# HGRN2 and short-convolution layer: diagonal blocks of A by identity products, and operands C in one run per partition

## The chip, the cores and the metric

The kernel runs on one core of one Trainium2 chip. The metric is the device time of one execution in microseconds (us), the median of several runs. Lower is better. The engines are TensorE (PE in the profile, with its weight loads as PEld), VectorE (DVE), ScalarE (ACT), GpSimd (POOL) and the queue that issues most DMAs (SP).

## What is computed

One layer works on 2048 tokens of width 1024, with 256 context tokens ahead of them. The tokens are normalised and modulated, and one input projection (1024 to 9216 columns) feeds two branches: a gated linear recurrence of 8 heads of width 128, run forward and backward, and a gated short convolution over rows of 64 tokens. Both go through one output projection. Cut to what matters here:

```python
def chunk_scan(q, k, v, logf, s0):                  # per head; chunks of tokens
    diff = bcum[:, :, :, None, :] - bcum[:, :, None, :, :]
    decay = where(mask, exp(where(mask, diff, 0)), 0)
    attn = einsum('bhtk,bhsk,bhtsk->bhts', qc, kc, decay)
    o = einsum('bhts,bhsv->bhtv', attn, vc) + einsum('bhtk,bhkv->bhtv', qc * exp(bcum), S)

p = h @ w_in[l]                                     # one projection for both branches
y = concatenate([hgrn_out(o, gate), conv_branch(p[..., HG_COLS:], conv_w, grid=True)]) @ w_out[l]
x = x + gate * y                                    # then a final RMSNorm
```

## The kernel before, in words

**Large products.** The projections run as products of f16 pairs (a high and a low part, three matmuls for one), put together after Strassen with 7 products instead of 8. A function `seven` issues the 7 products of a unit, `HK` = 4 k-tiles times 3 matmuls each. In the head windows a moving operand has 256 columns and comes from a tile `hop`; in the pair windows, where two token groups of 512 run together, it has 512 columns and comes from a tile `C[i][o]`, one for each of the 7 operands and 2 token halves.

**Order of the work.** Windows follow each other: 32 head windows (8 heads times 4 token groups, up to about 1262 us), 4 windows of the first convolution block, 14 pair windows for the other 7 blocks, then 8 output units. While a window's products are issued, the steps of other work (the scan of the segment of the window before, output steps of the head before, preparation of weights) are put between them by weights in a table `PACE`. The compiler's scheduler then sets the order on each engine from the program's order and its own account of when operands are there; each engine runs its queue in that order.

**A segment's scan.** A segment is 512 tokens (4 chunks of 128) of a head. Its attention matrix A is made in levels: at each level DVE multiplies decay totals into K (line 485) and Q (line 492), ACT and POOL keep mixed copies `km` and `qm` (lines 601 and 608), and PE makes blocks of A (line 631, 128x32 weights and 32 columns, 16 matmuls at a time). Levels 0 to 4 give the 32x32 diagonal blocks; DVE puts them together in a tile `Ac` of 128 partitions by 4 chunks by 32 (line 639). The step `level6` makes the last two levels in one PSUM bank `s.pt`: 16 matmuls of 64 columns for level 5 (line 650), which also write over the place of the diagonal blocks, and 16 for level 6 (line 657). ACT copies the bank to A (line 661), and POOL then copies the diagonal blocks out of `Ac` over it, 4 copies of 32 partitions (line 665). Two steps later the output products read A (line 737). Between them stand `key_turn` (transposes `kT` of K, line 672), `states` (products `T`, line 681) and, of the head before, output sums (line 777) whose banks come from the same pair of buffers as `kT`.

**Operands of the pair windows.** `load_C` loads each C by two DMAs, one for each token group (line 991). The source is 4096 bytes in one run per partition; the tile is laid out `[P, HK, 2, GW]`, so that a DMA writes 8 runs of 512 bytes in each partition. After the pair windows the same tiles hold the output weights (`wo_home`, `wo_at`, `load_wo`).

Of the kernel before, what the change touches and what calls it, by code (L numbers as in the profile page):

```python
# [10 lines left out]
F16 = mybir.dt.float16  # L11
# [8 lines left out]
P = 128  # L20
# [5 lines left out]
GW = 512  # L26
NG = SEQ // GW
NCH = GW // P
HK = KT // 2
HW = GW // 2  # L30
# [7 lines left out]
SB = 32  # L38
# [22 lines left out]
def hybrid_layer(ctx: ExitStack, tc, x, cx, w_ada, b_ada, w_in, w_out, fnorm_w, small_d, masks, ident_d, sel_d, out):  # L61
    nc = tc.nc
    V, S, G, PE, SY = nc.vector, nc.scalar, nc.gpsimd, nc.tensor, nc.sync
# [16 lines left out]
    OPS = ("B11", "T1", "T2", "B21", "T3", "B22", "T4")  # L80
# [3 lines left out]
    Hd = [{o: Hr[g][r][:, i] for r in ROWS for i, o in enumerate(r)} for g in range(NG)]  # L84
# [9 lines left out]
    def pa_t(nm):  # L94
        return pa.tile([P, 512], F32, tag="pa", name=nm)
# [4 lines left out]
    def ring(nm):  # L100
        return rp.tile([P, GW], F32, tag="ring", name=nm)
# [69 lines left out]
    ident = cp.tile([P, P], F32, name="ident")  # L171
# [335 lines left out]
    class Seg:  # L507
# [133 lines left out]
        def level6(s):  # L641

            n = s.n
            km, qm = s.kept
            s.pt = pa_t(f"A5_{s.nm}")
            for ch in range(NCH):
                for j in range(P // SB):
                    o = ch * P + j * SB
                    c0 = ch * P + j // 2 * 2 * SB
                    PE.matmul(s.pt[j * SB:(j + 1) * SB, c0:c0 + 2 * SB], km[:, o:o + SB], qm[:, c0:c0 + 2 * SB],  # L650
                              start=True, stop=True)
            for ch in range(NCH):
                for j in range(P // SB):
                    i = j // 2
                    o = ch * P + j * SB
                    t = ch * P + (1 - i) * 64
                    PE.matmul(s.pt[j * SB:(j + 1) * SB, t:t + 64], s.K[:, i * n + o:i * n + o + SB],
                              s.qf[:, (1 - i) * n + t:(1 - i) * n + t + 64], start=True, stop=True)
            s.update(6)
            s.A = ring(f"A_{s.nm}")  # L660
            S.activation(s.A, s.pt, AF.Copy)  # L661
            A3 = s.A.rearrange("p (c t) -> p c t", c=NCH)
            for j in range(P // SB):
                js = slice(j * SB, (j + 1) * SB)
                G.tensor_copy(A3[js, :, js], s.Ac[js])  # L665

        def key_turn(s):
            s.kT = []
# [300 lines left out]
    def finish_unit():  # L969
        while pending:  # L970
            pending.pop()()
        while afterwards:
            afterwards.pop(0)()


    late, ext = W(), W()
    late.rs = cp.tile([P, 33], F32, name="wrs")
    C = [{}, {}]
# [7 lines left out]
    def load_C(names, pool=None, tp=0):  # L986

        def one(o, j):
            if j == 0:
                C[tp][o] = (pool or ext.cr).tile([P, HK, 2, GW], F16, name=f"C{tp}{o}")  # L990
            SY.dma_start(C[tp][o][:, :, :, j * HW:(j + 1) * HW], Hd[2 * tp + j][o])

        return [lambda o=o, j=j: one(o, j) for o in names for j in range(2)]

# [13 lines left out]
    def settle(wk):  # L1008

        while any(j_[1] == wk for j_ in jobs):  # L1010
            for _ in jobs.pop(0)[2]:
                pass
# [13 lines left out]
    Wd = {o: dp.tile([P, 2, KT, GW], F16, name=f"Wd{o}", tag=f"Wd{o}") for o in OPS}  # L1026
# [32 lines left out]

    def wo_home(name, hl):  # L1060
        i = 2 * OPS.index(name) + hl
        return C[i // 7][OPS[i % 7]]

    def wo_at(name, hl, k):
        return wo_home(name, hl)[:, k // 2, k % 2, :]

    def load_wo(lo_, hi_):

        for i in range(lo_, hi_):
            SY.dma_start(wo_home(OPS[i // 2], i % 2).rearrange("p a k n -> p (a k) n"), Wd[OPS[i // 2]][:, i % 2])  # L1070

    Gr = dp.tile([P, GW], F32, name="Gr", tag="Gr")

# [124 lines left out]
    for hd in range(HEADS):  # L1198
# [4 lines left out]
        for i, g in enumerate(order(h.prim, NG)):  # L1203
            s = Seg(hd, g * GW, GW, 0, f"{hd}_{g}")
# [22 lines left out]
    for wi, (kind, a, i) in enumerate(stretch):  # L1227
# [69 lines left out]
        if kind == "head" and a >= 6:  # L1297
            n = (a - 6) * NG + i
            extra += [paced(0.2, lambda k=k: wo_scan(k)) for k in (2 * n, 2 * n + 1)]
        if kind == "pair":  # L1300
            n = (a - 1) * 2 + i
# [149 lines left out]
    ui = 0  # L1451

    def run(wi, units, steps):
# [20 lines left out]
        for un, (wk, kind, i, fn) in enumerate(units):  # L1474
            settle(wk)
            w = ws[wk]
            if not hasattr(w, "sx"):
                finish_w(w, f"w{ui}")
            final = turnover and kind != "ctx" and all(u[1] == "ctx" for u in units[un + 1:])
            def retire(wk=wk, at=ui):  # L1480
                if last[wk] == at:
                    next_w(wk[2], 4)

            if kind == "ctx":
                finish_unit()
                ps = bank(turn_bank[0], f"u{ui}")[:, :CTX]
                turn_bank[0] = 1 - turn_bank[0]
                for k in range(KT):
                    op, kk = w.ops[(("A11", "A12"), ("S1", "A22"))[i - 1][k // HK]], k % HK
                    r = k // HK * i  # L1490
                    PE.matmul(ps, op[0][:, kk], hc[:, r, 0, kk], start=k == 0, stop=False)
                    PE.matmul(ps, op[0][:, kk], hc[:, r, 1, kk], start=False, stop=False)
                    PE.matmul(ps, op[1][:, kk], hc[:, r, 0, kk], start=False, stop=k == KT - 1)
                    tick(1)
                fn(ps, w)
                retire()
            elif kind == "plain":
                ps = bank(turn_bank[0], f"u{ui}")
                turn_bank[0] = 1 - turn_bank[0]
                for half in range(2):  # L1500
                    hs = slice(half * HW, (half + 1) * HW)
                    for k in range(KT):
                        op, kk = w.ops[f"A{i}{k // HK + 1}"], k % HK
                        r = [plain[wi][k // 2][:, k % 2, hl, hs] for hl in range(2)]
                        PE.matmul(ps[:, hs], op[0][:, kk], r[0], start=k == 0, stop=False)
                        PE.matmul(ps[:, hs], op[0][:, kk], r[1], start=False, stop=False)
                        PE.matmul(ps[:, hs], op[1][:, kk], r[0], start=False, stop=k == KT - 1)
                        tick(1)
                fn(ps, w)
                retire()  # L1510
            elif kind == "pair":
                def pair_step(o, last_unit=ui == len(uses) - 1):
                    tick(2)
                    if o and last_unit and o != OPS[6]:
                        load_wo(7 + OPS.index(o), 8 + OPS.index(o))

                seven(w.ops.get, lambda o, hl, k, i=i: C[i][o][:, k, hl, :], HK, GW, f"{ui}", pair_step,
                      w.sx[:, 0:1], ring, retire, *fn(w))
            else:
                def step(o, final=final):  # L1520
                    tick(1)
                    if o and final:
                        freed[0] += 1
                        prefetch()

                seven(w.ops.get, lambda o, hl, k: hop[gw][o][:, k, hl, :], HK, HW, f"{ui}", step,
                      w.sx[:, 0:1], u_tile, retire, *fn(w))
            ui += 1
# [156 lines left out]
```

## Time and profile before

| | us |
|---|---|
| median of 3 runs | 2150.0 |
| lowest and highest of them | 2148.01, 2152.14 |
| the profiled execution | 2151.83 |
| its span, first to last instruction | 2150.1 |

A row of the profile gives an engine, a source line, what is written and read (out<-in), and times. In the timeline a group of equal instructions is one row with its count; an f32 matmul has two records, so that 16 of them show as x32. Durations of PE's instructions overlap, so what a group costs PE is read from its start to the start of the next. A wait is written as `[idle before <-releaser]`. The chain of work that ended last follows each instruction back to what released it.

### The profile page before, as it was taken

How to read it: one execution, taken by the hardware profiler on the slowest of the kernel's cores; microseconds unless marked ns; L12 is line 12 of the kernel's file. 1: busy time of each engine (PE TensorE's matmuls, PEld its weight loads, DVE VectorE, ACT ScalarE, POOL GpSimd, SP SyncE). 2: the span in 40 equal slices, each digit the busy share in tenths (PEclk: the TensorE clock that was granted, in tenths of full speed). 3: DMA queues.
4: the chain of work that ended last, by engine and by line, in shares of the span. 5: the costliest groups of instructions: out<-in, count | busy, mean ns of one | idle time of the engine just before them, and what ended most of it. 6: DMA issues, size and time to landing. Idle time of an engine off the chain costs nothing.

```text
span 2150.1 us, 53050 instructions
## 1 busy us (share of the span) xinstructions
PE 2073.2 (96%) x22111; PEld 1466.0 (68%) x22111; DVE 1645.8 (77%) x3413; ACT 1192.2 (55%) x2406; POOL 191.8 (9%) x272
## 2 busy tenths in 40 slices
PE   5988999999999999999999999999999999999998
PEld 2877878888888888888888887444444444444443
DVE  6787988878778787788687887678778656687775
ACT  7965666757567666576676654354445423333332
POOL 0121111111111110111110100000000000000000
PEclk9999999999999999999999999999999999999999
DMA  9567533442344233424543458933442105642421
GB/s 356 191 207 265 178 126 134 137 158 72 114 129 146 97 114 109 153 81 142 194 131 127 130 165 260 285 108 110 134 149 93 54 23 196 206 143 92 137 79 59
DMA packets 185798, 311.02 MB, mean 145 GB/s; under 512 B 13010, under 2 KB 114770, under 8 KB 183764
## 3 DMA queue, kind: packets, MB, share of 16 engines
q1 hardware_dynamic: 183396, 303.68, 42.9%
q8 instruction: 173, 2.83, 0.5%
q10 hardware_dynamic: 2160, 3.93, 0.5%
q14 instruction: 69, 0.57, 0.1%
HBM read 240.19 MB, written 67.37 MB: 143 GB/s over the span
## 4 chain that ended last, share of the span: by engine, by line
PE 65%; DVE 18%; ACT 7%; DMA 4%; issue 3%; POOL 1%; SPq 0%; POOLq 0%; ACTq 0%; DVEq 0%
PE sa L930 8%; PE sa L932 8%; PE sa L931 8%; PE sb L930 4%; PE sb L932 4%; PE sb L931 4%; PE sa_o L930 2%; PE sa_o L931 2%; PE sa_o L932 2%; DVE Q L492 2%; PE sc L930 2%; PE sc L931 2%; PE sc L932 2%; DVE K L485 2%; PE T L681 2%
## 5 line engine op out<-in xcount | busy, mean ns | idle before, releaser
L931 PEld LDWEIGHTS <-e_p 128*128 128x128 f16 x1332 | 130.4, 98 | 59.8 <-issue 10.3
L930 PEld LDWEIGHTS <-e_p 128*128 128x128 f16 x1332 | 130.4, 98 | 54.0 <-issue 1.1
L601 ACT ACTIVATE km<-K 128x512 f32<-128x512 f32 x192 | 129.6, 675 | 67.2 <-DVE K L485 61.1
L932 PEld LDWEIGHTS <-e_p 128*128 128x128 f16 x1332 | 130.3, 98 | 51.4
L485 DVE TENSOR_TENSOR K<-K,tot 128x512 f32<-128x512 f32 x192 | 132.2, 689 | 42.9 <-ACT km L601 25.3
L492 DVE TENSOR_TENSOR Q<-Q,tot 128x512 f32<-128x512 f32 x192 | 132.5, 690 | 34.9 <-POOL qm L608 19.5
L608 POOL COPY qm<-Q 128x512 f32<-128x512 f32 x96 | 80.8, 842 | 794.4 <-DVE Q L492 778.7
L931 PEld LDWEIGHTS <-whib_p 128*128 128x128 f16 x888 | 86.9, 98 | 42.1 <-issue 8.8
L930 PEld LDWEIGHTS <-whib_p 128*128 128x128 f16 x888 | 86.8, 98 | 36.7 <-issue 0.8
L930 PEld LDWEIGHTS <-whia_p 128*128 128x128 f16 x888 | 87.0, 98 | 35.7 <-DMA hop3B<-Hd3B 2.3
L932 PEld LDWEIGHTS <-wloa_p 128*128 128x128 f16 x888 | 87.0, 98 | 34.2
L931 PEld LDWEIGHTS <-whia_p 128*128 128x128 f16 x888 | 87.0, 98 | 33.9 <-issue 1.5
L932 PEld LDWEIGHTS <-wlob_p 128*128 128x128 f16 x888 | 86.8, 98 | 34.0
L157 ACT ACTIVATE e_p<-ws_p,sc_p 128x512 f16<-128x512 f32 x108 | 77.5, 718 | 54.9 <-DVE ws_p L444 42.0
L665 POOL COPY A<-Ac 32x128 f32<-32x128 f32 x128 | 77.2, 603 | 128.3 <-ACT A L661 110.6
L853 ACT ACTIVATE cv<-c,small 128x512 f32<-128x512 f32 (+1 forms) x36 | 24.2, 673 | 106.8 <-DVE c L871 61.1
L937 ACT ACTIVATE u<-sa,sx_w 128x256 f32<-128x256 f32 (+1 forms) x111 | 58.1, 524 | 43.5 <-PE sa L932 34.7
L937 ACT ACTIVATE p<-sa,sx_w 128x256 f32<-128x256 f32 (+1 forms) x111 | 57.4, 517 | 39.9 <-PE sa L932 39.8
L158 DVE SCALAR_TENSOR_TENSOR e_p<-ws_p,sc_p,e_p 128x512 f16<-128x512 f32 x108 | 79.4, 750 | 0.0
L409 ACT ACTIVATE junk<-ws_p 128x1024 f16<-128x1024 f32 x72 | 75.7, 1052 | 6.5 <-DMA ws_p<-in_w_in 6.3
L1596 POOL TENSOR_TENSOR x_o<-x_o,fw 128x512 f32<-128x512 f32 x1 | 1.3, 1262 | 868.0 <-ACT junk L1587 868.0
L937 ACT ACTIVATE p<-sb,sx_w 128x256 f32<-128x256 f32 (+1 forms) x111 | 57.8, 521 | 30.8 <-PE sb L932 28.0
(858 smaller groups left out, 7036.3 us busy)
## 6 DMA issues: line engine op xcount, KB each, us to landing
ws_p<-in_w_in SPq DMA_DIRECT2D x72, 512.0 KB, 4.3
y_o<-yT SPq DMA_DIRECT2D x32, 512.0 KB, 4.3
xt_x<-in_x SPq DMA_DIRECT2D x16, 512.0 KB, 6.2
wa<-in_w_ada SPq DMA_DIRECT2D x16, 512.0 KB, 10.2
Gd<-zs SPq DMA_DIRECT2D x32, 256.0 KB, 2.7
sg<-Gd SPq DMA_DIRECT2D x32, 256.0 KB, 4.4
wos<-in_w_out SPq DMA_DIRECT2D x32, 256.0 KB, 5.0
yT<-y SPq DMA_DIRECT2D x32, 256.0 KB, 2.9
```

The lines of the kernel that those rows point to most:

```text
L157: S.activation(hi, src, AF.Copy, scale=st[:, 0:1])
L158: V.scalar_tensor_tensor(lo, src, st[:, 0:1], hi, ALU.mult, ALU.subtract)
L409: S.activation(junk.rearrange("p (k n) -> p k n", k=KT), stage[i], AF.Abs, accum_out=r)
L485: V.tensor_tensor(m, m, sub(cur, nb + 1, [[2, np_], [-(nb + 1), 2], [0, B]]), ALU.mult)
L492: V.tensor_tensor(m, m, sub(cur, 1, [[2, np_], [nb - 1, 2], [0, B]]), ALU.mult)
L601: S.activation(sub(s.km, 0, [[2 * B, n // (2 * B)], [B, 2], [1, B]]), mix(s.K, n, B, n // (2 * B)), AF.Copy)
L608: G.tensor_copy(sub(qm, 0, [[2 * B, n // (2 * B)], [B, 2], [1, B]]), mix(s.qf, n, B, n // (2 * B)))
L665: G.tensor_copy(A3[js, :, js], s.Ac[js])
L930: PE.matmul(ps, hi[:, k], rh, start=start and k == 0, stop=False, skip_group_check=not start)
L931: PE.matmul(ps, hi[:, k], right(name, 1, k), start=False, stop=False, skip_group_check=not start)
L932: PE.matmul(ps, lo[:, k], rh, start=False, stop=k == nk - 1, skip_group_check=not start)
L937: last_keep.append(S.activation(r, ps, AF.Copy, scale=sx))
```

## The change

In `level6` 16 products are added behind those of line 657: columns `js` of the identity as weights, the chunk of `Ac` as moving operand, written into the bank over the diagonal blocks. ACT's copy of the bank then gives the whole of A, and the four copies on POOL are taken out. The tiles C are laid out `[P, 2, HK, 2, HW]`, with the token group outside, so that each DMA writes one run of 4096 bytes per partition; the moving operand of a pair product then is two runs of 256 columns. The views of the output weights in these tiles are rewritten for the new layout; their runs stay as they were.

```diff
@@ -656,13 +656,14 @@
                     t = ch * P + (1 - i) * 64
                     PE.matmul(s.pt[j * SB:(j + 1) * SB, t:t + 64], s.K[:, i * n + o:i * n + o + SB],
                               s.qf[:, (1 - i) * n + t:(1 - i) * n + t + 64], start=True, stop=True)
+            for ch in range(NCH):
+                for j in range(P // SB):
+                    js = slice(j * SB, (j + 1) * SB)
+                    PE.matmul(s.pt[js, ch * P + j * SB:ch * P + (j + 1) * SB], ident[:, js], s.Ac[:, ch], start=True,
+                              stop=True)
             s.update(6)
             s.A = ring(f"A_{s.nm}")
             S.activation(s.A, s.pt, AF.Copy)
-            A3 = s.A.rearrange("p (c t) -> p c t", c=NCH)
-            for j in range(P // SB):
-                js = slice(j * SB, (j + 1) * SB)
-                G.tensor_copy(A3[js, :, js], s.Ac[js])
 
         def key_turn(s):
             s.kT = []
@@ -987,8 +988,8 @@
 
         def one(o, j):
             if j == 0:
-                C[tp][o] = (pool or ext.cr).tile([P, HK, 2, GW], F16, name=f"C{tp}{o}")
-            SY.dma_start(C[tp][o][:, :, :, j * HW:(j + 1) * HW], Hd[2 * tp + j][o])
+                C[tp][o] = (pool or ext.cr).tile([P, 2, HK, 2, HW], F16, name=f"C{tp}{o}")
+            SY.dma_start(C[tp][o][:, j], Hd[2 * tp + j][o])
 
         return [lambda o=o, j=j: one(o, j) for o in names for j in range(2)]
 
@@ -1059,15 +1060,15 @@
 
     def wo_home(name, hl):
         i = 2 * OPS.index(name) + hl
-        return C[i // 7][OPS[i % 7]]
+        return C[i // 7][OPS[i % 7]].rearrange("p j k l n -> p (j k l n)").rearrange("p (k n) -> p k n", n=GW)
 
     def wo_at(name, hl, k):
-        return wo_home(name, hl)[:, k // 2, k % 2, :]
+        return wo_home(name, hl)[:, k, :]
 
     def load_wo(lo_, hi_):
 
         for i in range(lo_, hi_):
-            SY.dma_start(wo_home(OPS[i // 2], i % 2).rearrange("p a k n -> p (a k) n"), Wd[OPS[i // 2]][:, i % 2])
+            SY.dma_start(wo_home(OPS[i // 2], i % 2), Wd[OPS[i // 2]][:, i % 2])
 
     Gr = dp.tile([P, GW], F32, name="Gr", tag="Gr")
 
@@ -1514,7 +1515,7 @@
                     if o and last_unit and o != OPS[6]:
                         load_wo(7 + OPS.index(o), 8 + OPS.index(o))
 
-                seven(w.ops.get, lambda o, hl, k, i=i: C[i][o][:, k, hl, :], HK, GW, f"{ui}", pair_step,
+                seven(w.ops.get, lambda o, hl, k, i=i: C[i][o][:, :, k, hl, :], HK, GW, f"{ui}", pair_step,
                       w.sx[:, 0:1], ring, retire, *fn(w))
             else:
                 def step(o, final=final):
```

The order of PE at level 6 of the segment that the rows below show (head 2, group 0) was this, `hop9T` and `whib_p` being operands of the large products:

```order
L932 MATMUL sa_6430<-hop9T_6165,wlob_p_5603 128x256
L650 MATMUL A_2_0_6744<-qm_2_0_6727,km_2_0_6688 32x64 x16
L657 MATMUL A_2_0_6744<-Q_0_6221,K_0_5632 32x64 x16
L930 LDWEIGHTS whib_p_5602
L930 MATMUL sa_6430<-hop9T_6165,whib_p_5602 128x256
```

and is now this, with line numbers one higher behind the change:

```order
L933 MATMUL sa_6526<-hop9T_6261,wlob_p_5687 128x256
L650 MATMUL A_2_0_6840<-qm_2_0_6823,km_2_0_6784 32x64 x16
L657 MATMUL A_2_0_6840<-Q_0_6317,K_0_5716 32x64 x16
L662 MATMUL A_2_0_6840<-Ac_0_6607,ident 32x32 x16
L931 LDWEIGHTS whib_p_5686
L931 MATMUL sa_6526<-hop9T_6261,whib_p_5686 128x256
```

The new products stand right behind line 657, as in all 32 segments, and the large products follow them.

On DVE, behind the K and Q of that last level, stand the first instructions of the next segment (`Q_1`, `ks_1`, `K_1`, `tot_1`) and an output sum of the head before (`Q_3<-Q_3,o_1_3`, line 777). Before:

```order
L485 TENSOR_TENSOR K_0_5632<-K_0_5632,tot_0_6453 128x4x2x64
L492 TENSOR_TENSOR Q_0_6221<-Q_0_6221,tot_0_6453 128x4x2x64
L567 TENSOR_TENSOR Q_1_6790<-q_1_6429,f_1_6265 128x1024
L569 TENSOR_TENSOR ks_1_6792<-K_1_6266 128x512
L498 TENSOR_TENSOR tot_1_7001<-f_1_6265 128x512
L777 TENSOR_TENSOR Q_3_3842<-Q_3_3842,o_1_3_6819 128x512
L485 TENSOR_TENSOR K_1_6266<-K_1_6266,f_1_6265 128x256x2
```

Now:

```order
L485 TENSOR_TENSOR K_0_5716<-K_0_5716,tot_0_6549 128x4x2x64
L492 TENSOR_TENSOR Q_0_6317<-Q_0_6317,tot_0_6549 128x4x2x64
L569 TENSOR_TENSOR ks_1_6900<-K_1_6362 128x512
L567 TENSOR_TENSOR Q_1_6898<-q_1_6525,f_1_6361 128x1024
L485 TENSOR_TENSOR K_1_6362<-K_1_6362,f_1_6361 128x256x2
L498 TENSOR_TENSOR tot_1_7109<-f_1_6361 128x512
L778 TENSOR_TENSOR Q_3_3890<-Q_3_3890,o_1_3_6927 128x512
```

`K_1<-K_1,f_1` has moved ahead of the output sum, which is line 778 now; the same change of places is there in 6 segments. Beyond these, DVE has 40 evacuations of line 941 in other places (33 of them later, by one to three), 61 state sums of line 725 (53 later) and 65 multiplications of line 485 (42 earlier); ACT has 46 copies `km` in other places (39 earlier). PE's order is otherwise the same from the fourth head window on.

## Rows read from the trace of the kernel before

**Rows 1.** the page: engines' busy time, the chain's shares, two Pool groups

```profile
PE 2073.2 (96%) x22111; PEld 1466.0 (68%) x22111; DVE 1645.8 (77%) x3413; ACT 1192.2 (55%) x2406; POOL 191.8 (9%) x272
...
PE 65%; DVE 18%; ACT 7%; DMA 4%; issue 3%; POOL 1%; SPq 0%; POOLq 0%; ACTq 0%; DVEq 0%
...
L608 POOL COPY qm<-Q 128x512 f32<-128x512 f32 x96 | 80.8, 842 | 794.4 <-DVE Q L492 778.7
...
L665 POOL COPY A<-Ac 32x128 f32<-32x128 f32 x128 | 77.2, 603 | 128.3 <-ACT A L661 110.6
```

**Rows 2.** busy us by stretch: PE, PEld, DVE, ACT, POOL, granted clock, DMA

```profile
300.00:1262.00 962.00, 940.09 (x14476) 830.42 (x14475) 769.68 (x1696) 631.70 (x1426) 132.51 (x187) 1.00 0.39 128
...
1345.00:2150.00 805.00, 794.15 (x3682) 358.28 (x3679) 573.87 (x995) 313.42 (x478) 4.16 (x3) 1.00 0.38 124
```

**Rows 3.** what PE waited for, 300 to 1262 us: total us, times, longest us

```profile
PE A L631 <- POOL qm L608: 6.9, 8, 2.7
PE sa L930 <- ACT u L937: 3.3, 11, 0.6
PE A L631 <- DVE Q L492: 2.1, 8, 0.3
...
PE kT L672 <- DVE Q L777: 1.0, 4, 0.2
```

**Rows 4.** who waited for the copies of line 665: us, times

```profile
  POOL hpT_x L301: 2.0, 1
```

**Rows 5.** timeline of PE at level 0: start us, us, line, tiles, shape

```profile
422.93 0.46 PE L631 MATMUL A<-q,ks 128*32 128x32 f32 x32
423.20 0.56 PE L631 MATMUL A<-Q,km 128*32 128x32 f32 x32
423.70 0.28 PE L930 MATMUL sa<-hop9T,whib_p 128*128 128x256 f16 x1
```

**Rows 6.** timeline of PE at level 6 of the same segment

```profile
435.48 0.65 PE L650 MATMUL A<-qm,km 128*32 128x64 f32 x32
435.95 0.63 PE L657 MATMUL A<-Q,K 128*32 128x64 f32 x32
436.51 0.28 PE L930 MATMUL sa<-hop9T,whib_p 128*128 128x256 f16 x1
```

**Rows 7.** pieces of the chain behind level 6: start us, us, what

```profile
436.13 0.49 PE A L657 x32
...
436.64 0.69 DVE K L485
...
440.55 0.60 DVE Q L777
441.15 1.04 DVE K L485
```

**Rows 8.** timeline of PE after it, in brackets the wait and what ended it

```profile
441.20 0.66 PE L672 MATMUL kT<-ident,K 128*128 128x128 f32 x4 [0.25 <-DVE Q L777]
...
457.36 0.46 PE L631 MATMUL A<-qm,km 128*32 128x32 f32 x32 [0.46 <-POOL qm L608]
458.09 0.46 PE L631 MATMUL A<-Q,km 128*32 128x32 f32 x32 [0.27 <-DVE Q L492]
```

**Rows 9.** timeline of the SP queue at the last loads of C

```profile
1351.46 2.76 SPq L991 DMA_DIRECT2D C1T<-Hd3T  x1
...
1369.44 1.17 SPq L401 DMA_DIRECT2D ws_p<-in_w_in  x1
```

**Rows 10.** what PE waited for, 1262 to 2150 us, the longest

```profile
PE sa L930 <- DVE b L941: 0.9, 1, 0.9
```

**Rows 11.** timeline of Pool and DVE behind level 6

```profile
437.30 3.41 POOL L665 COPY A<-Ac 32x128 f32<-32x128 f32 x4 [3.63 <-ACT A L661]
...
439.09 0.77 DVE L569 TENSOR_TENSOR ks<-K 128x512 f32<-128x512 f32 x1
```

**Rows 12.** all of line 569: ns min/median/max, first and last start

```profile
L569 DVE TENSOR_TENSOR ks<-K x32: 676/688/1097, 72.7 to 1235.9; 128x512 f32<-128x512 f32 x32
```

## Prediction

> **What bounds the kernel now.** I read the page's busy shares and chain first, then busy time by stretch, then what TensorE waited for in each stretch, and last the timeline around one level 6 step. TensorE (PE) is busy for 2073.2 us of a span of 2150.1 us [rows 1]. By stretch it is busy for 940.09 of the 962 us from 300 us to the end of the head windows, and for 794.15 of the 805 us of the pair and output windows, at a granted clock of 1.00 in both [rows 2]. So PE sets the end, and work that is added to its queue costs its full length unless it falls into a wait that PE has anyway. Such waits are few: from 300 to 1262 us PE waits 6.9 us in 8 places for the Pool copy qm, 3.3 us in 11 for an evacuation u, 2.1 us in 8 for Q, and 1.0 us in 4 for Q of line 777 [rows 3]. The chain names PE with 65% and DVE with 18% [rows 1]: DVE is on it only in those few stretches that end in one of these waits.
>
> **Edit 1, what is removed.** 128 copies on Pool, 77.2 us [rows 1]. Nobody waits for them but one other Pool instruction, for 2.0 us once [rows 4]. The output products that read A come two steps later and don't wait for Pool at all. So this part is worth nothing by itself. What DVE may gain from a quieter Pool is a rival, below.
>
> **Edit 1, what is added.** 16 products per segment, 32 segments, 512 in all, on the engine that sets the end. They stand right behind the 16 products of line 657, with no wait of their own, since Ac's last write on DVE comes ahead of the K and Q that line 657 waits for. Their form is that of line 631 (128x32 weights, 32 columns, f32), and a group of 16 shows as x32 in the timeline. Two such groups back to back start 0.27 us apart, and the second holds PE for 0.50 us until the next f16 product [rows 5]; a group that followed a wait held it for 0.39 us [rows 8]. Today the products of line 650 hold PE for 0.47 us, those of line 657, which end the f32 stretch, for 0.56 us [rows 6]. With a third group behind them line 657 should take 0.47, as line 650 does, and the new group 0.39 to 0.50: 0.47 + 0.39 - 0.56 = 0.30, or 0.47 + 0.50 - 0.56 = 0.41. I take 0.35 us, and 0.27 and 0.41 as ends. Times 32 that is **11.2 us** (8.6 to 13.1), if all of it is on the path.
>
> **Edit 1, where it is not on the path.** In the segment shown, DVE's K of the last level starts at 436.64, when line 657's reads end [rows 7]; it doesn't wait for the new products. 4.7 us later PE stands 0.25 us at a transpose kT for the bank that DVE's line 777 frees, and 16 us after that 0.46 and 0.27 us at the levels of the next segment [rows 8]. Here DVE leads and PE follows, so 0.35 us more on PE would be swallowed. PE stands at kT like this in 4 places [rows 3], and the program has the sequence in 6 of its 32 segments (it shows in the order of DVE, above). In the others I count the full 0.35 us.
>
> **What the new order does.** The scheduler has moved more than the new products. At these same 6 places K times f, which holds DVE for 1.04 us behind line 777 now [rows 7], stands ahead of it in the new order. The bank is then freed about 1.0 us later, and PE's kT with it: 1.0 us instead of the 0.35 us above, some 0.7 us more, times 6: **+4.2 us**. Later PE arrives so late at the levels that about 0.5 us of the 0.73 us there [rows 8] is gone, in each of the 6: **-3 us**; I keep 0 to -4.4 as ends, since on ACT the scalings of line 825 also move and two more of them stand ahead of the second gate. Waits that don't hang on PE elsewhere (the T products for kT, the early segments) may swallow 0.3 us each in some 8 segments: **-2.5 us** (0 to -4). Many evacuations (line 941) and sums (line 725) stand one or two places later, levels earlier; no row shows a wait that this moves, so I count 0 with 3 us on either side.
>
> **Edit 2, the operands C.** The 28 loads carry the same bytes in one run per partition. The late ones keep the SP queue for up to 2.76 us each now, and a weight load behind them is issued at 1369.44 [rows 9]. It should get shorter to issue and to land. But PE's whole waiting from 1262 us on has one entry above 0.5 us, 0.9 us for an evacuation on DVE, and none for a load [rows 10]. So this gain is hidden: 0, at most a few tenths. On PE the moving operand is now two runs of 256 columns instead of one of 512, in 14 windows x 2 units x 7 x 12 = 2352 products. In runs of one element a group of 16 took 0.56 against 0.46 us [rows 5], 6 ns each with 31 breaks, 0.2 ns per break; in runs of four it took the same 0.46 us as in one run [rows 8]. Two runs are nearer to the latter: 0, at most 2352 x 0.2 ns = 0.5 us.
>
> **The sum.** 11.2 + 4.2 - 3 - 2.5 = +9.9 us against the profiled execution of 2151.8 us. I take +9, since the two last terms could be larger more easily than the first. The three timed runs have their median 1.8 us below the profiled one, so the forecast for the median is 2150.0 + 9 = **2159 us**. What a measurement of this kernel can tell from no change is about 0.2%, 4.3 us; the forecast lies at 0.4%.
>
> **Rivals.**
> *Swallowed.* The new products fall into waits that PE has anyway. For: 21.9 us of the 962 us are not busy by [rows 2], about as much as the products add twice over. Against: 3.3 us of them are for evacuations u [rows 3], which follow PE's own last product and move with it. It would give +0 to +4 us, 2150 to 2154.
> *The order costs more.* Where K or km now stands ahead of an evacuation, PE waits for a bank not at 6 places but in most segments. Upper ends of the terms: 13.1 + 4.2 + 3 + 0.5 = 20.8, so 2165 to 2171. For: PE has 3.3 us of waits for u in 11 places already [rows 3], so the slack there is short. Against: the evacuations that move behind km are mostly p5 of bank b, which is needed again only two products later.
> *Faster: DVE is freed from Pool's copies.* Line 569 took 0.77 us while the copies of line 665 ran, from 437.30 to 440.71 us [rows 11], and has a median of 0.688 us over all segments [rows 12]. 77 us of copies cover at most some 110 instructions of that size, 0.08 us each: 9 us less on DVE. If the whole of the waits for qm, Q and line 777 (6.9 + 2.1 + 1.0 = 10.0 us [rows 3]) went with that, and all of the products fell into what is left of the idle time (21.9 - 10.0 = 11.9 us), the end would be 2150 - 10.0 = 2140 us. It decides from the point where more than 15.5 us of PE's idle time go (11.2 us for the products, and 4.3 us). Against: line 569 was itself waited for by nobody, and Pool stands idle for 778.7 us in total ahead of its qm copies, waiting for DVE's Q [rows 1], so those waits are not Pool's making. On this the Trainium skill, "SBUF — State Buffer", section "Who interferes with whom", says that VectorE and GpSimd share one pair of ports by an exclusive lock; by "SBUF: two separate sides" of that page the loser blocks fully. By that rule the copies could hold DVE for up to their whole 77 us, and the kernel would come out on this rival's side; the rows bear out at most the 0.08 us.
> *The change is not felt where it says.* Edit 2 may reach nothing since no load is waited for; that is already my count, and what would speak against it is a time that falls although the products cost what they cost.
>
> **How the numbers follow.** Forecast (+4 to +14) 0.48; swallowed 0.20; the order costs more 0.22; faster 0.10. The most likely gives 2159. Leaving out the faster case and the far half of the costlier one, the range is 2149 to 2169. Faster by over 0.2%: 0.09; within: 0.24 (swallowed, and a little of the two beside it); slower: 0.67.
>
> **What the profile of the changed kernel would show.** Line 662 with x1024 records and the line after it some 0.35 us later than before; no Pool copy to A; kT waiting for line 778 in 6 places for about a microsecond; the waits for qm near 457 us gone or smaller; loads of C at 0.3 to 0.6 us of SP each; pair products of the same length as now. A stretch from 300 to 1262 us that is not 6 to 12 us longer would make the prediction wrong, as would a change in the length of the pair windows.

## The result, and the profile after

The changed kernel takes 2158.78 us (median of 5 runs, 2157.59 to 2160.03) where the kernel before takes 2150.0 us (5 runs, 2146.92 to 2152.14): a ratio of 1.0044, interval 1.0033 to 1.0055. It is slower by over 0.2%. The forecast was 2159.0 us. The profiled execution took 2158.78 us with a span of 2157.0 us, 6.9 us more than the span before.

From the page of the changed kernel, the engines' busy time, the chain's shares, and two groups (busy us, mean ns of one, then idle time before them and what ended it):

```profile
PE 2078.2 (96%) x23135; PEld 1477.2 (68%) x23135; DVE 1643.9 (76%) x3413; ACT 1191.5 (55%) x2406; POOL 115.1 (5%) x144
...
PE 67%; DVE 16%; ACT 8%; DMA 4%; issue 3%; POOL 1%; SPq 0%; POOLq 0%; ACTq 0%; DVEq 0%
...
L608 POOL COPY qm<-Q 128x512 f32<-128x512 f32 x96 | 79.5, 828 | 978.5 <-DVE Q L492 978.5
...
L662 PE MATMUL A<-Ac,ident 128*32 128x32 f32 x1024 | 15.3, 197 | 0.0
```

Beside [rows 1]: POOL has lost its 77 us of copies, and the identity products have their 1024 records with no idle time ahead of them. By stretch (columns as in [rows 2]) the head windows carry the change:

```profile
300.00:1262.00 962.00, 938.19 (x15138) 833.97 (x15140) 760.94 (x1679) 628.15 (x1421) 68.43 (x82) 1.00 0.39 127
1345.00:2157.00 812.00, 801.10 (x3721) 362.26 (x3719) 579.47 (x1016) 316.66 (x483) 4.16 (x3) 0.99 0.37 125
```

PE is busy 1.9 us less in the first stretch than in [rows 2], although it has more to do there: it waits more. What it waited for, 300 to 1262 us (total us, times, longest us):

```profile
PE A L631 <- POOL qm L608: 6.5, 6, 2.6
PE sa L931 <- ACT u L938: 3.8, 11, 0.7
PE vt_c L555 <- ACT vT_c L550: 3.5, 3, 1.2
PE kT L673 <- DVE Q L778: 2.4, 4, 0.6
PE A L631 <- DVE Q L492: 2.1, 8, 0.3
```

Against [rows 3], kT waits 2.4 us in place of 1.0, and a wait that the prediction doesn't have stands third: the turn of the context values `vt_c`, 3.5 us in 3 places. PE's timeline at level 6 of the segment that [rows 6] shows:

```profile
434.65 0.65 PE L650 MATMUL A<-qm,km 128*32 128x64 f32 x32
435.12 0.63 PE L657 MATMUL A<-Q,K 128*32 128x64 f32 x32
435.57 0.48 PE L662 MATMUL A<-Ac,ident 128*32 128x32 f32 x32
435.98 0.28 PE L931 MATMUL sa<-hop9T,whib_p 128*128 128x256 f16 x1
...
441.04 0.66 PE L673 MATMUL kT<-ident,K 128*128 128x128 f32 x4 [0.61 <-DVE Q L778]
```

From line 657's start to the next f16 product it is 435.98 - 435.12 = 0.86 us now, 0.56 in [rows 6]: a group of 16 costs 0.30 us. The last row answers to the first of [rows 8]: 0.61 us of wait in place of 0.25.

**A stretch for comparisons.** Whole times scatter by some us from run to run, so beside the medians I compare one stretch that all kernels have: from the first product behind level 6 of head 1's first segment to the same of head 6's first, 20 segments. In PE's timeline of the kernel before, of the changed kernel, of the kernel without diagonal blocks (e3) and of the one with both orders put back (e12, lines as in the changed kernel; e3's are 5 lower), its ends are:

```profile
290.69 0.28 PE L930 MATMUL sa<-hop5T,e_p 128*128 128x256 f16 x1
1015.32 0.28 PE L930 MATMUL sa<-hop25T,whib_p 128*128 128x256 f16 x1
```

```profile
289.21 0.28 PE L931 MATMUL sa<-hop5T,e_p 128*128 128x256 f16 x1
1018.94 0.28 PE L931 MATMUL sa<-hop25T,whib_p 128*128 128x256 f16 x1
```

```profile
289.06 0.28 PE L926 MATMUL sa<-hop5T,e_p 128*128 128x256 f16 x1
1011.41 0.28 PE L926 MATMUL sa<-hop25T,whib_p 128*128 128x256 f16 x1
```

```profile
290.51 0.28 PE L931 MATMUL sa<-hop5T,e_p 128*128 128x256 f16 x1
1016.13 0.28 PE L931 MATMUL sa<-hop25T,whib_p 128*128 128x256 f16 x1
```

That is 724.63 us before, and 729.73, 722.35 and 725.62 us then: +5.1, -2.3 and +1.0 us against before. The other kernels, read in the same way from one profiled execution each, stand in the table.

| kernel | median us | ratio to before, interval | 20 segments, against before, us |
|---|---|---|---|
| changed | 2158.78 | 1.0044 (1.0033 to 1.0055) | +5.1 |
| e1 products alone | 2158.86 | 1.0051 (1.0037 to 1.0064) | +4.9 |
| e2 layout alone | 2147.89 | 1.0000 (0.9991 to 1.0010) | -0.5 |
| e3 no diagonal | 2144.80 | 0.9985 (0.9976 to 0.9993) | -2.3 |
| e4 products and copies | 2163.55 | 1.0070 (1.0057 to 1.0083) | +8.1 |
| e5 products first, narrow | 2147.35 | 0.9988 (0.9979 to 0.9997) | -1.8 |
| e6 narrow | 2156.38 | 1.0033 (1.0021 to 1.0045) | +4.9 |
| e7 sum first | 2157.05 | 1.0031 (1.0018 to 1.0045) | +3.4 |
| e8 products twice | 2185.18 | 1.0159 (1.0142 to 1.0176) | +18.7 |
| e9 turn first | 2157.10 | 1.0034 (1.0023 to 1.0045) | +2.6 |
| e10 copies on ACT | 2153.09 | 1.0011 (1.0001 to 1.0021) | +1.9 |
| e11 narrow and copies | 2158.27 | 1.0039 (1.0026 to 1.0053) | +3.1 |
| e12 both orders | 2156.56 | 1.0034 (1.0020 to 1.0049) | +1.0 |

The kernel before, run beside each group, had medians of 2148.02 (e1 to e4), 2150.04 (e5 to e8), 2149.21 (e9 to e11) and 2150.18 us (e12).

### The profile page after: what moved, and what is told of

Same layout as the page of the kernel before. It is cut to its first block, busy times and chain, and to the rows that moved or that the text cites. A ratio compares the mean times of both kernels' runs of the same rounds, so it can differ in the third digit from the quotient of the medians.

```text
span 2157.0 us, 54885 instructions
## 1 busy us (share of the span) xinstructions
PE 2078.2 (96%) x23135; PEld 1477.2 (68%) x23135; DVE 1643.9 (76%) x3413; ACT 1191.5 (55%) x2406; POOL 115.1 (5%) x144
## 4 chain that ended last, share of the span: by engine, by line
PE 67%; DVE 16%; ACT 8%; DMA 4%; issue 3%; POOL 1%; SPq 0%; POOLq 0%; ACTq 0%; DVEq 0%
PE sa L931 8%; PE sa L933 8%; PE sa L932 8%; PE sb L931 4%; PE sb L932 4%; PE sb L933 4%; PE sa_o L931 2%; PE sa_o L933 2%; PE sa_o L932 2%; PE sc L931 2%; PE sc L932 2%; PE sc L933 2%; DVE Q L492 2%; PE A L631 2%; PE T L682 2%
## 5 line engine op out<-in xcount | busy, mean ns | idle before, releaser
L157 ACT ACTIVATE hiS_o<-y_o,sc_y 128x1024 f16<-128x1024 f32 x32 | 36.8, 1149 | 70.1 <-PE sa_o L932 32.1
L682 PE MATMUL T<-v,kT 128*128 128x128 f32 x512 | 64.2, 278 | 2.6 <-ACT kT L675 2.5
```

The lines of the kernel that those rows point to most:

```text
L157: S.activation(hi, src, AF.Copy, scale=st[:, 0:1])
L682: PE.matmul(pt[:, sl], s.kT[i][:, sl], s.v[:, sl], start=True, stop=True)
```

## Experiments: the two edits and the copies on POOL

The theory was the prediction's: the products cost their time on PE, the new order a few us, the copies on POOL and the layout nothing. The rivals: the layout matters, or POOL's copies hold DVE.

**e1 and e2, one edit at a time.** Of the changed kernel, e1 takes back the layout, e2 the first hunk:

```diff
-                C[tp][o] = (pool or ext.cr).tile([P, 2, HK, 2, HW], F16, name=f"C{tp}{o}")
-            SY.dma_start(C[tp][o][:, j], Hd[2 * tp + j][o])
+                C[tp][o] = (pool or ext.cr).tile([P, HK, 2, GW], F16, name=f"C{tp}{o}")
+            SY.dma_start(C[tp][o][:, :, :, j * HW:(j + 1) * HW], Hd[2 * tp + j][o])
...
```

Expected of e1: 

> The first edit alone (identity products in, copies on POOL out), C laid out as before; every engine's order is that of the changed kernel. Theory (the products' own time on PE makes the loss, the layout of C is worth nothing): 2157 to 2160, as the changed kernel's 2158.8. Rival (the two-run moving operand of the pair products costs something): 2152 to 2156, with the missing 3 to 7 us coming out of the pair windows. Rival (the quicker loads of C hide part of the loss): 2161 to 2165.

Expected of e2: 

> The second edit alone (C in one run per partition), the diagonal blocks still copied by POOL; every engine's order is that of the kernel before. Theory (layout worth nothing): 2149 to 2152, pair products of the same length, loads of C at 0.3 to 0.6 us of SP each and no wait of PE changed. Rival (two-run operand costs): 2153 to 2157. Rival (loads of C were in the way of other transfers): 2143 to 2147.

e1 took what the changed kernel takes, e2 what the kernel before takes, to within 0.1%; e2's 2147.89 us lies below the range that the theory gave, but so does the kernel before beside it, with 2148.02. The whole loss is the first edit's. The pair windows say the same of the two-run operand. The first and the last of their products, before and then in the changed kernel:

```profile
1335.83 0.38 PE L930 MATMUL sa<-C0B,whia_p 128*128 128x512 f16 x1 [0.89 <-DVE b L941]
1854.42 0.38 PE L932 MATMUL sa<-C1T,wlob_p 128*128 128x512 f16 x1
```

```profile
1342.76 0.38 PE L931 MATMUL sa<-C0B,whia_p 128*128 128x512 f16 x1 [0.89 <-DVE b L942]
1861.38 0.38 PE L933 MATMUL sa<-C1T,wlob_p 128*128 128x512 f16 x1
```

That is 518.59 and 518.62 us. In the profiled execution of e2 it is 4.0 us more, with one wait of 2.16 us for ACT and a granted clock of 0.66 from 1835 to 1840 us; e3, which has the same layout, has 518.58. The loads of C did get shorter to issue, SP's timeline of the changed kernel at the place of [rows 9]:

```profile
1351.26 0.59 SPq L992 DMA_DIRECT2D C1T<-Hd3T  x1
```

0.59 us in place of 2.76, and nobody had waited for it.

**e3, neither products nor copies.** Of the changed kernel:

```diff
-            for ch in range(NCH):
-                for j in range(P // SB):
-                    js = slice(j * SB, (j + 1) * SB)
-                    PE.matmul(s.pt[js, ch * P + j * SB:ch * P + (j + 1) * SB], ident[:, js], s.Ac[:, ch], start=True,
-                              stop=True)
```

> The changed kernel without the identity products and without the copies on POOL: the diagonal 32x32 blocks of A are left out. Every engine's order is then that of the kernel before, so that against the layout alone only the 128 copies on POOL are missing. Theory (those copies cost nothing, since DVE is not held by them and A is read two steps later): 2149 to 2152. Rival (POOL's copies hold DVE or the output products): 2139 to 2145, and the changed kernel would then have hidden a gain of some 7 us behind a loss of some 16.

**e4, products and copies.** Of the changed kernel, behind ACT's copy:

```diff
+            A3 = s.A.rearrange("p (c t) -> p c t", c=NCH)
+            for j in range(P // SB):
+                js = slice(j * SB, (j + 1) * SB)
+                G.tensor_copy(A3[js, :, js], s.Ac[js])
```

> The changed kernel with the copies on POOL kept behind ACT's copy (they write the same blocks a second time); every engine's order is that of the changed kernel. Theory (copies cost nothing): 2157 to 2160, as the changed kernel. Rival (the copies hold DVE, and their removal repaid part of the products): 2163 to 2169.

Both went against the theory. e2 and e3 have the same order on every engine and differ in the copies alone: 2147.89 - 2144.80 = 3.1 us (1.8 us in the 20 segments). e1 and e4 differ in the same way within the other order: 2163.55 - 2158.86 = 4.7 us (3.3 us). By the scatter of the runs each of the two differences is known to some 2.5 us either way, and neither reaches down to zero. So the copies did cost something, 3 to 5 us, and their removal paid for part of the products. How, DVE's timeline behind level 6 of the same segment shows, in e2 and then in e3:

```profile
437.02 1.31 DVE L567 TENSOR_TENSOR Q<-q,f 128x1024 f32<-128x1024 f32 x1
438.25 0.77 DVE L569 TENSOR_TENSOR ks<-K 128x512 f32<-128x512 f32 x1
438.95 0.77 DVE L498 TENSOR_TENSOR tot<-f 128x512 f32<-128x512 f32 x1
439.64 0.67 DVE L777 TENSOR_TENSOR Q<-Q,o 128x512 f32<-128x512 f32 x1
```

```profile
435.73 1.22 DVE L567 TENSOR_TENSOR Q<-q,f 128x1024 f32<-128x1024 f32 x1
436.86 0.69 DVE L569 TENSOR_TENSOR ks<-K 128x512 f32<-128x512 f32 x1
437.46 0.68 DVE L498 TENSOR_TENSOR tot<-f 128x512 f32<-128x512 f32 x1
438.07 0.68 DVE L773 TENSOR_TENSOR Q<-Q,o 128x512 f32<-128x512 f32 x1
```

Three instructions in a row take 0.09 us longer each beside POOL's copies, and the output sum (line 777, line 773 in e3) comes 0.27 us earlier without them, measured from the start of the first row: 439.64 - 437.02 = 2.62, and 438.07 - 435.73 = 2.34. That sum is what kT waits for, so in these places the 0.27 us are PE's too: the kT entry of [rows 3], 1.0 us, is gone in e3. DVE's busy time falls by 1645.1 - 1640.5 = 4.6 us in all. The copies themselves, all 128 in e2 (ns min/median/max, first and last start):

```profile
L665 POOL COPY A<-Ac x128: 284/653/1466, 123.8 to 1260.5; 32x128 f32<-32x128 f32 x128
```

The shortest takes 0.28 us, the median 0.65; read one by one, those at 436 to 440 us each end 0.15 us after an instruction of DVE has ended. With DVE idle beside it a copy takes 0.29 us, so that about half of the 77 us is waiting for DVE (128 x 0.29 = 37 us are left), and each copy that got in held DVE up for 0.09 us. Not every instruction of DVE is held: in e2 line 569, both inputs of which lie in SBUF, takes 0.77 us in the 11 places with a copy beside it and 0.68 in the others, but the output sum of line 777, which reads a PSUM bank, takes 0.67 in 6 places beside a copy and 0.68 elsewhere.

## Experiments: products, place and order

**e5, products first and narrow.** Of the changed kernel; the identity products, unchanged, stand ahead of this:

```diff
-                    c0 = ch * P + j // 2 * 2 * SB
-                    PE.matmul(s.pt[j * SB:(j + 1) * SB, c0:c0 + 2 * SB], km[:, o:o + SB], qm[:, c0:c0 + 2 * SB],
+                    c0 = ch * P + (j ^ 1) * SB
+                    PE.matmul(s.pt[j * SB:(j + 1) * SB, c0:c0 + SB], km[:, o:o + SB], qm[:, c0:c0 + SB],
```

> The changed kernel with the identity products ahead of line 650 and with line 650's products 32 columns wide (only the blocks beside the diagonal, so that they don't write over it). The 16 narrow products should take about as long as the identity products, 0.27 to 0.30 us where line 650 takes 0.47. DVE's and ACT's orders are then nearly those of the kernel before. Theory A (the products' own time on PE, 9.4 us, is most of the loss): 2158.8 - 32 x 0.18 = 2153, less what of the products now falls into PE's waits for qm, 2150 to 2153. Theory B (the new order of the queues costs some 5 us, the copies on POOL gave back 3 to 5): both the order and the narrow blocks are won back, 2145 to 2149.

**e6, narrow.** The same lines, and the identity products stay last.

> The changed kernel with line 650's products 32 columns wide, and the identity products where the change has them. DVE's and ACT's orders are nearly those of the changed kernel. Both theories: 32 x (0.47 - 0.29) = 6 us less than the changed kernel, 2152 to 2154. Against the kernel with the products first it tells the order's price: theory A has them within 3 us of each other, theory B has this one 4 to 7 us slower.

e5 is as theory B has it, 11 us below the changed kernel, and the one kernel with the whole of A that is faster than both kernels, if by 0.1% only. e6 kept most of the loss, more than either theory gave it. In segments without other waits both have the products' price as expected: e6 and e5 lose 0.12 us a segment against before, the changed kernel 0.30. But e6 gave this back: in head 5's last segment PE waits 0.46 us for a gate and 0.78 us for qm of line 650, which it doesn't in the changed kernel. Between e5 and e6 stand the products' place and the order of DVE and ACT (e5's is nearly that of before). No run changes one of the two alone, but the 20 segments show where the 6.7 us between them lie: 4.9 us in the seven segments in which e6 waits for kT or for `vt_c` and e5 doesn't (e7 and e9, below, price the same waits at 1.5 and 2.6 us), and 1.8 us in head 5's last segment. So most of it goes with the order.

**e7, sum first.** Of the changed kernel:

```diff
-            level_k(s.K, s.cur, n, lev)
+            follow(late_sums[-1:] if lev == 0 and s.tok0 == (1 + s.hd % 2) * GW else [], lambda: level_k(s.K, s.cur, n, lev))
...
-            V.tensor_tensor(s.o, s.o, po, ALU.add)
+            late_sums.append(V.tensor_tensor(s.o, s.o, po, ALU.add))
```

> The changed kernel, with K times f of line 485 held behind the output sum of line 778 in the second segment of each of heads 2 to 7, as in the kernel before; PE's order is that of the changed kernel. The prediction's step (the late sum costs 0.7 us in each of 6 places): 4 us less than the changed kernel, 2154 to 2156. Rival (the kT waits of 0.61 us where 0.25 stood, in 4 places, are all): 0 to 1.5 us less, 2157 to 2159.

1.7 us less by the medians and in the 20 segments, the rival's side. The kT waits are gone from PE's list, and four segments are 0.36 to 0.38 us shorter.

**e9, turn first.** Why `vt_c` waits shows in ACT's and then PE's timeline of the changed kernel:

```profile
407.82 0.68 ACT L601 ACTIVATE km<-K 128x512 f32<-128x512 f32 x1 [1.02 <-DVE K L485]
408.40 0.46 ACT L550 ACTIVATE vT_c<-u,sx_w 128x256 f32<-128x256 f32 x1
```

```profile
407.42 0.27 PE L932 MATMUL sa<-hop9B,whia_p 128*128 128x256 f16 x1
408.91 0.44 PE L555 MATMUL vt_c<-ident,vT_c 128*128 128x128 f32 x2 [1.22 <-ACT vT_c L550]
```

The products u that vT_c reads were done at 406.8, but ACT's queue has a km of level 1 ahead of it, and that km waits 1.02 us for DVE's K. PE's next item in its queue is the transpose of vT_c. In the kernel before, vT_c stands ahead of that km. The edit, of the changed kernel:

```diff
-            S.activation(s.vT[:, :s.n], ps[:, :s.n], AF.Copy, scale=w.sx[:, s.m:s.m + 1])
+            turns.append(S.activation(s.vT[:, :s.n], ps[:, :s.n], AF.Copy, scale=w.sx[:, s.m:s.m + 1]))
...
-                s.mixed(lev + 1)
+                follow(turns[-1:] if lev == 0 and s.tok0 == 0 and s.hd in (2, 4, 6) else [], lambda: s.mixed(lev + 1))
```

> The changed kernel, with ACT's copy km of level 1 held behind its copy vT_c (line 550) in the first segment of heads 2, 4 and 6, as in the kernel before; 36 rows of PE's order and 8 of ACT's move, nothing else of note. Theory (in the changed kernel PE waits 3.5 us at 3 places for vT_c, because ACT's queue has a km ahead of it that waits for DVE): the three waits fall to about 0.1 us and the time by 3 us, 2155 to 2157. Rival (the waits only stand in for others that come next): no change, 2158 to 2160.

The three waits are gone, and the three segments get 0.77, 0.79 and 1.00 us shorter: +2.6 in place of +5.1 us over the 20 segments. The median, 2157.10 us, is 1.7 us below the changed kernel's and 0.1 us above the theory's range. The same two engines in e9, ACT and then PE:

```profile
409.18 0.47 ACT L550 ACTIVATE vT_c<-u,sx_w 128x256 f32<-128x256 f32 x1
410.08 0.68 ACT L601 ACTIVATE km<-K 128x512 f32<-128x512 f32 x1 [0.43 <-DVE K L485]
```

```profile
409.70 0.44 PE L555 MATMUL vt_c<-ident,vT_c 128*128 128x128 f32 x2
```

**e12, both orders back.** The edits of e7 and e9 together.

> The changed kernel with both of the orders before put back: K times f behind the output sum (6 places) and km behind vT_c (3 places). Theory (the loss is 9.4 us of products and some 5 us of order, less 3 to 5 us that POOL's copies gave back): the kT waits give back 1.5 us and the vT_c waits 2.6 us, both together 4 us less than the changed kernel, 2153 to 2156, and 9 us or more above the kernel without diagonal blocks. Rival (the waits are exchanged for others): 2157 to 2159, no less than with either order alone.

In the 20 segments the two add up: +1.0 us, 4.1 less than the changed kernel (1.7 and 2.4). The median, 2156.56 us, doesn't show it: it lies 0.5 us below those of e7 and e9, with an interval of some 3 us either way, one of its 8 runs being at 2164.98. So the sum is shown for the stretch, and for the whole time only that it isn't contradicted.

**e8, products twice.** A second loop with the same 16 products behind the first.

> The changed kernel with the 16 identity products issued a second time into the same place. Theory A (0.295 us of PE for each group, in every segment on the path): 9 us more than the changed kernel, 2166 to 2169. Rival (much of them is swallowed where DVE leads): 2161 to 2165. More than 2171 would show that an order which changes again decides.

Far above both, the third case. In plain segments the step is 0.59 us, twice 0.295, so the price of the products holds; that makes 11.8 of the +18.7 us in the 20 segments. The rest goes with waits of a third order. The whole time has more: e8 comes to the 20 segments 12.3 us later than the changed kernel, and what costs it that was not followed up. PE's list for 300 to 1262 us:

```profile
PE oT L837 <- ACT kT L680: 7.6, 5, 1.5
PE A L631 <- POOL qm L608: 4.4, 5, 1.6
PE sa L936 <- ACT u L943: 3.7, 11, 0.6
PE kT L678 <- DVE Q L783: 3.3, 6, 0.7
PE T L687 <- ACT kT L680: 2.5, 4, 1.1
```

**e10 and e11, other ways to the same blocks.** e10 has ACT make the four copies; e11 has line 650 narrow, and ACT copy the bank in 6 pieces around the diagonal, POOL's copies kept. e10, of the kernel of e2:

```diff
-                G.tensor_copy(A3[js, :, js], s.Ac[js])
+                S.activation(A3[js, :, js], s.Ac[js], AF.Copy)
```

e11, of the kernel of e2 with e5's narrow products:

```diff
-            S.activation(s.A, s.pt, AF.Copy)
+            for i in range(2):
+                S.activation(A3[64 * i:64 * i + 64, :, 64 - 64 * i:128 - 64 * i],
+                             p3[64 * i:64 * i + 64, :, 64 - 64 * i:128 - 64 * i], AF.Copy)
+            for j in range(P // SB):
+                x = (j ^ 1) * SB
+                S.activation(A3[j * SB:(j + 1) * SB, :, x:x + SB], p3[j * SB:(j + 1) * SB, :, x:x + SB], AF.Copy)
```

> The kernel with the new layout of C, no identity products, and the four diagonal copies issued on ACT in place of POOL; the orders of DVE and ACT are otherwise those of the kernel before. Theory (POOL's copies lengthen what DVE does beside them, 0.09 us an instruction, and that costs 3 us; ACT has room behind its copy of the bank): 2145 to 2149 where the kernel before has 2148 to 2150. Rival (ACT's 4 copies of some 0.25 us hold the evacuations that follow): 2152 to 2158.

> The kernel with the new layout of C, no identity products, line 650's products 32 columns wide, the copies of the diagonal on POOL as before, and ACT's copy of the bank in 6 pieces that leave the diagonal out. Theory: PE has 32 x 0.18 = 6 us less than before, DVE is held by POOL as before: 2142 to 2146. Rival (ACT's six pieces hold its evacuations, or the new order costs as it did in the changed kernel): 2149 to 2156.

e10 went to its rival; e11, with 2158.27 us, lies above even its rival's range. What PE waited for, 300 to 1262 us, in e10 and then in e11:

```profile
PE sa L930 <- ACT u L937: 5.0, 14, 0.7
PE T L681 <- ACT kT L674: 4.1, 7, 1.4
```

```profile
PE T L686 <- ACT kT L679: 6.5, 9, 1.7
PE sa L935 <- ACT u L942: 4.6, 12, 1.1
```

ACT is busy for 57% of the span in both, yet the state products T wait for its copy of kT for 4.1 and 6.5 us (1.3 us in 3 places in e3): the pieces stand between level 6 and that copy in ACT's queue. At 613.28 us in e10 the four copies take 1.25 us, two evacuations and the copies of kT follow, and T waits 0.44 us for them; at the same place in e3 T doesn't wait.

## Why the prediction was right, and where not

The time, the sign and the main term hold. That the median came out within 0.3 us of the forecast is luck: the products were counted somewhat too high, and of the other terms several were wrong in opposite ways. Over the 20 segments (the prediction's terms are for all 32) the runs put the change together as -2.3 (copies gone, e3) + 5.9 (products, 20 x 0.295) - 2.6 (of these swallowed) + 1.7 (kT, e7) + 2.4 (vT_c, e12 against e7) = +5.1 us; the swallowed part is not measured by itself, it is what e12 lacks: -2.3 + 5.9 - 1.0. The remaining 1.8 us of the profiled spans' 6.9 lie beside the stretch. The changed kernel comes to it 1.5 us earlier (from 135 to 145 us the kernel before ran at a granted clock of 0.82 to 0.83 and the changed kernel at 1.00, which is 1.7 us; the other differences there go both ways); it takes 3.3 us more for the 7 segments behind it; and from the last segment's level 6 to the end both take 888.4 us. Neither of the signs of being wrong came: from the same start to that last level 6 it is 979.4 us in place of 971.0, 8.4 more, and the pair windows kept their length.

- **Copies worth nothing: wrong.** The step that failed is "nobody waits for them, so this part is worth nothing by itself". They were worth 3.1 us (e2, e3) and 4.7 us (e1, e4), through DVE. The rival had the mechanism and the size of one hit (0.08 us, measured 0.09) and was set aside because line 569 was waited for by nobody. But the instructions behind line 569 in DVE's queue are late by the sum of the hits, and kT waits for the last of them. The rival's 9 us and its fall to 2140 didn't come either. On the Trainium skill's rule of the exclusive lock ("SBUF — State Buffer", section "SBUF: two separate sides", by which whoever comes second blocks) the trace agrees for POOL, with copies of 0.29 us that took 0.65 in the median beside DVE. What DVE loses is less than a lone copy, 0.09 us for each that got in, and about half of POOL's 77 us, the bound that the prediction set for DVE's loss, was POOL's own waiting.
- **Products: right.** 0.295 us a group (0.35 taken, 0.30 to 0.41 worked out), 9.4 us for 32 in place of 11.2. The lower of the two sums from [rows 5, 6, 8] was the true one.
- **Swallowed where DVE leads: wrong as put.** The 0.25 us that PE waits for kT ahead of the second segments [rows 8] was to swallow the products there. But that wait was made by POOL's hits on DVE: in e3 it is gone, and the second segments are 0.3 us shorter than before. It can be used once only. With both orders back (e12) these four segments cost 0.32 to 0.35 us more than in e3, the full price.
- **kT late: right in kind, too big.** 0.61 us of wait in 4 places, not 1.0 in 6; +1.7 us by e7 where 4.2 stood. The sum on DVE moved by 0.95 us of K times f, as said, but 0.27 us of that came back from the hits that POOL no longer makes, the term counted at nothing. With POOL's copies kept (e4), PE's list from 300 to 1262 us has the prediction's picture:

```profile
PE kT L677 <- DVE Q L782: 4.6, 6, 1.0
```

- **Levels get back 3 us: right in kind, too big.** The total of the waits for qm hardly moved, 6.9 to 6.5 us, and that for Q stayed at 2.1 [rows 3]. But in the four segments in which kT is late the qm waits fell from 0.46, 0.24, 0.46 and 0.42 us to 0.19 and 0.20 in two and to nothing that the list shows in the others, 1.2 us in all; in head 7 they grew. Head 2's second segment adds up so: 0.30 for the products, 0.61 - 0.25 for kT, less 0.46 - 0.19 for qm is 0.39, and it is 0.39 us longer. Most of this is no term beside e7's 1.7 us: with kT's order put back the four waits are 0.25 to 0.32 us again. What stood in the place of these 3 us in the sum, by chance of about the same size, was the copies' share.
- **Swallowed elsewhere, 2.5 us: right in size, in other places than named.** The last segments of heads 1, 3 and 5 are 0.21, 0.56 and 0.53 us shorter in e12 than in e3, although e12 has the products, and head 4's first is 0.36 us shorter, where a wait of T for kT, 0.64 us, is gone. With the products' 0.295 us, 0.5, 0.9, 0.8 and 0.7 us are swallowed there; the other 16 segments give 0.2 us more than the products' price. Which waits take up the products in those last segments was not followed up.
- **No wait behind the km that move: wrong.** The section on the change lists 46 moved km, and the prediction counted 0 with 3 us on either side, for want of a row. Three of them stood ahead of vT_c and cost 2.4 us in the stretch. The question that would have found them: what stands behind each moved instruction that itself waits, and is PE next in line for it.
- **Layout of C: right.** 2147.89 against 2148.02 us, and pair windows of the same length.

## What to carry to other kernels

A few products more on the engine that sets the end cost their plain length, and that could be read to some 0.05 us a group from the start-to-start times of their neighbours; the order that a planner makes around them can cost as much again, so look in the new order for instructions that wait and have moved ahead of short ones that the bounding engine needs next. Copies on POOL that nobody waits for are not free where the bounding engine waits for the end of DVE's queue. When an operation is added, try it in two places: the same products, ahead of the step that waits for qm, made a kernel 9 us faster than behind it (e5, e6), mostly by the order that came with the place.

## What was not expected of the hardware

**A clock that falls or not.** In head 6's second segment PE waits for a qm in every kernel, 1.5 to 2.7 us, and the granted clock at and behind that wait differs from one profiled execution to the next. The changed kernel (busy us by engine, then granted clock, DMA share, GB/s) and then e3:

```profile
1040.00:1045.00 5.00, 2.62 (x72) 2.00 (x73) 3.74 (x9) 5.00 (x17) 1.74 (x2) 0.80 0.84 281
1045.00:1050.00 5.00, 5.00 (x99) 4.13 (x97) 3.65 (x7) 1.66 (x5) 0.00 (x0) 0.86 0.32 97
```

```profile
1030.00:1035.00 5.00, 2.23 (x78) 1.69 (x76) 3.13 (x5) 5.00 (x15) 1.13 (x1) 1.00 0.85 293
1035.00:1040.00 5.00, 5.00 (x107) 4.42 (x104) 4.86 (x10) 3.10 (x9) 0.61 (x1) 1.00 0.40 130
```

The wait ended at 1042.11 us after 2.62 us in the first and at 1033.84 after 2.50 in the second; the clock stood at the lower of its two levels (1.2 and 2.4 GHz) for a part of those windows in the first alone. That segment is 2.5 to 2.6 us shorter in e3, e7 and e9 than in the changed kernel; by the granted clock of the two windows 1.7 us of that are the clock's (5 x 0.20 + 5 x 0.14). The length of the wait doesn't decide it: the clock fell in 8 of the 14 profiled executions, with waits of 1.6 to 2.7 us (2.66 in the kernel before), and not in the other 6, with waits of 1.5 to 2.65 (e4). What does, no run here tells, and as each kernel was profiled once, whether it differs between runs of one kernel isn't shown. This is why the 20 segments end ahead of it.

**POOL beside DVE.** A copy of 32x128 on POOL took 0.29 us alone and 0.65 in the median; a DVE instruction of 0.685 us with two inputs in SBUF took 0.77 beside it. Beside DVE instructions that read a PSUM bank neither side was held in e2: a copy took 0.285 to 0.287 us in nine places beside an evacuation of line 941, and line 941 0.475 us with a copy and 0.477 without.
